# Rotary embedding in two stored parts, added on GpSimd where queries and keys are read

## Chip, cores and metric

One core of a Trainium2 chip runs one step of a hybrid layer (differential attention beside a state-space scan, then a feed-forward part). The metric is the time of one execution on the device in microseconds (us), the median of the runs.

The core has a tensor engine (TensorE, PE in the profile; PEld is its weight load), a vector engine (VectorE, DVE), a scalar engine (ScalarE, ACT), GpSimd (POOL) and SyncE (SP), which in this kernel issues nearly all DMA transfers. Each engine works through its own instructions in the order of the program and waits for the others by semaphores.

## What is computed

The part of the reference that the change touches. Queries and keys are cut out of one projection; the rotary embedding is a sum of two products, and it is made for the 1024 latent tokens alone, not for the 128 context tokens.

```python
def apply_rope(x, cos, sin):
    return x * cos + rotate_half_axial(x) * sin

proj = h @ w_in                      # columns: q | k | v | u, 512 each
q_in, keys = apply_rope(q, ...), apply_rope(k, ...)
keys = concatenate([ctx_k, keys])    # 128 cached context keys, 1024 latent keys
s = einsum(q_blk, k) * scale         # 4 heads, two maps each
p = softmax(s)
w = p[:, :, 0] - lam * p[:, :, 1]
attn = rmsnorm(einsum(w, v))
# beside it: u -> bidirectional complex scan -> gelu -> gated unit
# then: output projection, residual, feed-forward
```

## The kernel before

Tokens stand in nine tiles of 128 rows: tiles 0 to 7 are latent, tile 8 (`CH`) is the context. All matrix products are made from split operands (a high and a low part), so three products stand for one.

The input projection (`win_mm`, lines 455 to 466) goes over chunks of 256 columns in the order u, v, k, q, two chunks each, and over the nine tiles in each chunk: one step is 24 products of 128x256 into one PSUM tile, of which there are three. One step later `win_evac` (468 to 503) empties it. For values and for context rows that is a copy on ACT into `st`. For latent rows of keys and queries DVE does four things: the product with the cosines into `rt` (line 488), the two products with the sines into `st` (493, 494), and the add of the two in place (495). `st` is a ring of three tiles, `rt` a single one. The store of `st` to a scratch tensor in DRAM (`q_s`, `k_s`, `v_s`; line 498) is put in the list `later` and issued on SP in the next round; from step 49 on the evacuation stands after the first products of a step, and its store one step later.

The order of all engines' work is written out by hand: the loop at line 1318 interleaves the projection's steps with a side generator, `front_side`. While values are projected, it builds the scans' matrices; while keys and the first queries are projected, it runs the scans (`ssm_pipe`, lines 918 to 1072: transposes and products on PE, rotations and scans on DVE, adds on GpSimd at 983 and 1008); and beside the last queries it reads the keys (`kv_steps`, 1175 to 1214), followed in part by the split of the gated unit's input (line 1231).

`kv_steps` goes over ten tiles: the context's keys, the cached keys, then latent tiles 0 to 7. `load` (line 1182) fetches 256 KB into `kin`, a ring of two; `split` makes the high part on ACT (1196) and the low part on DVE (1197) and then asks for the tile after next; PE transposes the split tile (1209) and ACT copies it into the key matrix (1213). One projection step takes two such tiles.

Attention works in units (token tile, head), four to a tile. The query tile is loaded by `q_load` (1374, `qin`, a ring of two), split by `q_split` on ACT (1380) and `q_low` on DVE (1388) with two copies on GpSimd (1390), and transposed for the next tile (`q_trans`). The load of a tile is asked for in one unit, and the split comes in the unit after. Beside it the output projection's weights are split, high part on ACT (1504, `woh`) and low part on GpSimd (1505, `wol`); in a unit of the loop at line 1597 this stands ahead of `q_split`.

Of the kernel before, what the change touches and what calls it, by code (L numbers as in the profile page):

```python
# [20 lines left out]
P = 128  # L21
D = 1024
KD = D // P
ATT = 512
# [33 lines left out]
def tile_hybrid_step(  # L58
# [39 lines left out]
    q_s = [dr.tile([P, ATT], F32, name=f"q_s{t}") for t in range(NT)]  # L98
    k_s = [dr.tile([P, ATT], F32, name=f"k_s{t}") for t in range(NT)]
    v_s = [dr.tile([P, ATT], F32, name=f"v_s{t}") for t in range(NT)]  # L100
    u_c = dr.tile([P, ATT], F32, name="u_c")
# [43 lines left out]
    def rsqrt1s(pl, cols):  # L145
        """The inverse root of some columns, divided by RS."""
        ts = []
        for ss, scale, tag in cols:
            v, y, f = [pl.tile([P, 1], F32, tag=tag + n, name=tag + n) for n in "vyf"]
            yi = pl.tile([P, 1], I32, tag=tag + "i", name=tag + "i")  # L150
            ts.append([v, y, f, yi, yi.bitcast(F32)])
        for (v, y, f, yi, cur), (ss, scale, tag) in zip(ts, cols):
            if scale is None:
                V.tensor_scalar(v, ss[:, 0:1], ss[:, 1:2], EPS, ALU.add, ALU.add)
            else:
                V.tensor_scalar(v, ss, scale, EPS, ALU.mult, ALU.add)  # L156
        for v, y, f, yi, cur in ts:
            V.tensor_single_scalar(yi, v.bitcast(I32), 1, op=ALU.logical_shift_right)
        for v, y, f, yi, cur in ts:
            V.tensor_scalar(yi, yi, -1, 0x5F3759DF, ALU.mult, ALU.add)  # L160
        for c in (-3.0, -12.0, -768.0):
            for v, y, f, yi, cur in ts:
                V.tensor_scalar(f, cur, cur, v, ALU.mult, ALU.mult)  # L163
            for x in ts:
                v, y, f, yi, cur = x
                V.scalar_tensor_tensor(y, f, c, cur, ALU.add, ALU.mult)  # L166
                x[4] = y
        return [x[1] for x in ts]
# [18 lines left out]

    # ------------------------------------------------------------- pools for the first part
    pst_es, pst = pool("pst", space=PSUM)
# [17 lines left out]

    # ------------------------------------------------------------- loads
    wm_raw = {}
# [6 lines left out]
    def load_wm0(j, n):  # L216
        """Half of a quarter of the first shift's (n even) or scale's columns."""
        if j % 2 == 0:
# [94 lines left out]
    load_wm0(1, 3)  # L313
    # ------------------------------------------------------------- modulation, statistics, normalised input
    def mod_mm(ps, c0, nq, k):
# [18 lines left out]

    # ------------------------------------------------------------- statistics of the rows
    TG = [(0, 4), (4, 8), (8, 9)]
# [52 lines left out]

    # ------------------------------------------------------------- input and output maps, state on the partitions  # L390
    prm = pb.tile([P, NQ, 4, 8, GC], F32, name="prm")
# [56 lines left out]

    # ------------------------------------------------------------- input projection
    u_sb = [su.tile([P, 8, CH, GC], F32, name=f"u_sb{o}") for o in range(4)]  # L450
# [17 lines left out]
    def win_evac(c0, t, ps):  # L468
        if c0 >= 1536:
# [5 lines left out]
            else:  # L475
                st = p1c.tile([P, NW], F32, tag="st", bufs=3, name="st")
                A.copy(st, ps)
                later.append(lambda: DMA.dma_start(u_c[:, cu:cu + NW], st))
            return
        st = p1c.tile([P, NW], F32, tag="st", bufs=3, name="st")  # L480
        sec, cq = c0 // ATT, c0 % ATT
        if sec == 2 or t == CH:
            A.copy(st, ps)
        else:
            t1 = p1c.tile([P, NW], F32, tag="rt", bufs=1, name="rt")
            nh = NW // HD
# [7 lines left out]
            V.tensor_mul(s5[:, 1], p5[:, 0], r5)  # L494
            V.tensor_add(st, st, t1)
        dst = (q_s, k_s, v_s)[sec][t]
        def store():
            DMA.dma_start(dst[:, cq:cq + NW], st)
            if t == CH and sec:
                o = (None, new_k, new_v)[sec].rearrange("a b t h e -> (a b t) (h e)")  # L500
                DMA.dma_start(o[:, cq:cq + NW], st)

        later.append(store)

    # ------------------------------------------------------------- the start

# [12 lines left out]
    def mod_out(j):  # L519
        """Shifts and scales of two blocks of channels."""  # L520
        rows = mod_rows(psm0.pop(j))
# [26 lines left out]

    # small things
    ones2 = pp.tile([P, 2, NS], F32, name="ones2")  # L550
# [305 lines left out]

    # ------------------------------------------------------------- maps of the scans, four groups of a direction at a time
    def after(f):
# [57 lines left out]

    # ------------------------------------------------------------- scans, four groups at a time
    def ssm_pipe(sp, Q):
# [177 lines left out]
    class Pipe:  # L1096
        """Staggered generators: a new one every `every` steps, each moved on once a step."""

# [15 lines left out]

    # the rest of the modulation, a quarter of its columns at a time
    MSEC = (2048, 3072, 4096, 5120)
# [54 lines left out]

    # ------------------------------------------------------------- keys
    kvd = {}

    def kv_steps(ktp):
        kins = {}

        def load(t):
# [3 lines left out]
            DMA.dma_start(kin, src)  # L1182
            kins[t] = kin

        seq = [CH, -1] + list(range(CH))
# [17 lines left out]
        for n, t in enumerate(seq):  # L1203
            split(n + 1)
            ks = kss.pop(n)
            for h2 in range(2):
# [8 lines left out]

    # ------------------------------------------------------------- gated unit
    zsp = {}
# [91 lines left out]

    # ------------------------------------------------------------- the projection, with the rest beside it  # L1310
    tm_es = None
# [34 lines left out]
    p1_es.close()  # L1346
    # ------------------------------------------------------------- attention
    def rsqrt_pool(pl, ss, n, scale, tag, bufs=1, split=False):
# [23 lines left out]
    def q_load(t):  # L1372
        qin = pa.tile([P, 2 * NH, HD], F32, tag="qin", bufs=2, name="qin")
        DMA.dma_start(qin, q_s[t].rearrange("p (h e) -> p h e", e=HD))
        tl_[t] = dict(qin=qin)

    def q_split(t, late=False):
# [159 lines left out]

    # ------------------------------------------------------------- gated unit
    gl_es, gl = pool("gl", side="left")
# [17 lines left out]

    # the context's queries go beside the unit's products
    def ctx(m):
# [12 lines left out]
    for n in range(3):  # L1572
        next(gms)
        if n == 1:
            q_split(CH)
            q_load(order[2])
    for h in range(NH):
        q_trans(CH, h)
# [18 lines left out]
    for i in range(NH - 2, N):  # L1597
# [31 lines left out]
        if j < N:  # L1629
# [6 lines left out]
            if tj + 1 < NT:  # L1636
                q_trans(order[tj + 1], h)
            if h == NH - 1 and tj + 2 < NT:
                q_split(order[tj + 2], True)
            if i >= NH - 1:  # L1640
# [36 lines left out]

    # ------------------------------------------------------------- output projection, second norm
    mx_load(order[1])
# [24 lines left out]

    # quarters of the second part's input: half of the tokens, half of its columns, half of that half of tokens
    quart = [{n: slot(f"r{4 * b + i}", dt=F32) for i, n in enumerate(("A11", "A12", "A21", "A22"))} for b in range(2)]
# [73 lines left out]

    # weights of the second part's inputs: quarters, their sums, split
    raw, wop = {}, {}
# [178 lines left out]

    # ------------------------------------------------------------- feed-forward: gate and up parts
    psf_es, psf_ = pool("psf", space=PSUM)
# [13 lines left out]
    def prod(f, i, b):  # L1977
        """One of the seven products of a block, and the sums that it completes."""
        u = un.setdefault((f, b), {})
# [125 lines left out]

    # ------------------------------------------------------------- feed-forward: second product
    HEAD = 1
# [36 lines left out]

    # the seven products of a pair of rows' tiles, of columns' halves and of token tiles (q, q + 4)
    def w2_load(p):
# [5 lines left out]
    def w2_tasks(p):  # L2152
        """Sums in place and splits: rows' tiles (0, 1), columns' halves (0, 1)."""
        at = {1: (0, 0), 7: (0, 1), 2: (1, 0), 3: (1, 1), 5: (2, 0), 6: (2, 1), 4: (1, 0)}
# [68 lines left out]
    def mm2(ps, s, p, n, ix, start, stop):  # L2223
        """Passes of one product: tokens' operand ix by the rows' operand n."""
        h, l = [t[1][:, ix] if isinstance(ix, int) else t[1][:, ix[0], ix[1]] for t in g2[s]]
# [282 lines left out]
def _rope_tables():  # L2508
    """Rotary tables of the token grid (shapes alone), rows ordered as the token tiles are:
    partition p of tile j holds token p * CH + j; the sine of an axis once for both halves."""  # L2510
    tok = (np.arange(P)[:, None] * CH + np.arange(CH)[None, :])
# [30 lines left out]
```

## Time and profile before

| | us |
|---|---|
| median of three runs | 1561.98 |
| lowest and highest of them | 1559.31, 1562.66 |
| the profiled execution, span from first to last instruction | 1562.2 |
| PE busy in it | 1451.2 |
| DVE busy | 1177.3 |
| ACT busy | 677.4 |
| POOL (GpSimd) busy | 534.6 |

The profile is one execution on the chip. Its page gives the span, the busy time of each engine, and the busy tenths of each engine in 40 equal slices of the span. Further views group instructions by line, list who waited for whom, cut the span into stretches, or print instructions in order of time. A tile's name stands on the left of its inputs (`ks<-kin`). "Idle before" is the time for which an engine did nothing ahead of an instruction, and the name behind the arrow is what ended it. Rows of an engine with a "q" behind its name belong to its sequencer, which issues DMA transfers and waits.

### The profile page before, as it was taken

Reading aid. Unit: us, or ns where it says so; the run is one execution under the profiler, and the core shown is the slowest. Engines: PE = TensorE matmul, PEld = TensorE weight load, DVE = VectorE, ACT = ScalarE, POOL = GpSimd, SP = SyncE. Lnnn points to the kernel's source line nnn. Section 1 sums busy time; section 2 is a strip of 40 time slices with the busy share of each in tenths; the row PEclk is TensorE's granted clock in tenths of the full one; section 3 lists DMA queues with packets and bytes.
Section 4 is the critical chain, followed back from the end, with each engine's and each line's share of the span. In section 5 each row is a group of like instructions: output and inputs, shape, how many; then the busy total and the mean of one; then the engine's idle time right before and its main releaser. Section 6 shows DMA issues by size and latency. Waiting matters only on the chain. (4 is left out here: it accounts for less than half of the span.)

```text
span 1562.2 us, 27432 instructions
## 1 busy us (share of the span) xinstructions
PE 1451.2 (93%) x10331; PEld 1326.9 (85%) x10331; DVE 1177.3 (75%) x2049; ACT 677.4 (43%) x1381; POOL 534.6 (34%) x656
## 2 busy tenths in 40 slices
PE   4879998989999999989879999999999999999986
PEld 3867797888989999868779999999999996888765
DVE  5579839997558888648797666666666678898988
ACT  2443255542658887536652223222322236333322
POOL 1355417774113442321440000000000017786866
PEclk9879999999999999989999999999999999999998
DMA  9329944333442111055412222222222123333325
GB/s 294 117 80 334 338 156 120 109 114 111 126 147 80 48 49 35 8 159 166 121 42 75 81 79 72 67 82 78 72 67 81 58 94 106 107 115 106 123 94 189
DMA packets 162452, 175.70 MB, mean 112 GB/s; under 512 B 18080, under 2 KB 132720, under 8 KB 162320
## 3 DMA queue, kind: packets, MB, share of 16 engines
q1 hardware_dynamic: 161392, 173.24, 34.8%
q8 instruction: 82, 1.34, 0.4%
q10 hardware_dynamic: 816, 0.57, 0.1%
q0 software_dynamic: 112, 0.13, 0.1%
q14 instruction: 50, 0.41, 0.1%
HBM read 128.70 MB, written 45.20 MB: 111 GB/s over the span
## 5 line engine op out<-in xcount | busy, mean ns | idle before, releaser
L1984 PE MATMUL m<-l,wh 128*128 128x288 f32 x1320 | 276.7, 296 | 5.5 <-DVE l L1712 4.4
L1984 PE MATMUL m<-r,wh 128*128 128x288 f32 x1144 | 241.5, 297 | 3.4 <-DVE rav L156 3.0
L1984 PEld LDWEIGHTS m<-l,wh 128*128 128x128 f32 x1320 | 215.6, 189 | 6.6 <-DVE l L1712 4.9
L1984 PE MATMUL m<-l,wl 128*128 128x288 f32 x704 | 208.4, 296 | 2.9 <-DVE wl L1801 2.9
L1984 PEld LDWEIGHTS m<-r,wh 128*128 128x128 f32 x1144 | 188.0, 189 | 4.2 <-DVE r L1712 4.0
L463 PE MATMUL ps_in<-wh,hh 128*128 128x256 f32 x576 | 179.7, 312 | 5.0 <-DVE hh L385 4.1
L465 PE MATMUL ps_in<-wh,hl 128*128 128x256 f32 x576 | 167.4, 291 | 5.5 <-DVE hl L388 5.5
L464 PE MATMUL ps_in<-wl,hh 128*128 128x256 f32 x576 | 167.3, 290 | 0.7 <-DVE wl L272 0.7
L2162 POOL TENSOR_TENSOR l<-r 128x512 f32<-128x512 f32 x2 | 3.0, 1521 | 452.8 <-DMA r<-in_w_ffn_out_dram 452.8
L1984 PE MATMUL m<-r,wl 128*128 128x288 f32 x528 | 157.1, 298 | 0.2 <-DVE wl L1801 0.2
L1800 ACT CAST wh<-raw 128x512 fp32r<-128x512 f32 x132 | 77.8, 621 | 147.4 <-DVE raw L1826 117.6
L463 PEld LDWEIGHTS ps_in<-wh,hh 128*128 128x128 f32 x576 | 114.6, 199 | 25.3 <-issue 18.9
L1984 PEld LDWEIGHTS m<-l,wl 128*128 128x128 f32 x704 | 133.1, 189 | 3.1 <-DVE wl L1801 3.1
L1801 DVE TENSOR_TENSOR wl<-raw,wh 128x512 fp32r<-128x512 f32 x132 | 93.3, 708 | 38.5 <-ACT wh L1800 38.4
L465 PEld LDWEIGHTS ps_in<-wh,hl 128*128 128x128 f32 x576 | 114.4, 199 | 6.5 <-DVE hl L388 6.4
L464 PEld LDWEIGHTS ps_in<-wl,hh 128*128 128x128 f32 x576 | 115.0, 200 | 1.1 <-DVE wl L272 1.1
L1424 DVE TENSOR_REDUCE mx<-S 128x1 f32<-128x1152 f32 (+1 forms) x72 | 88.7, 1236 | 22.1 <-PE S L1421 21.8
L1984 PEld LDWEIGHTS m<-r,wl 128*128 128x128 f32 x528 | 100.3, 190 | 0.5 <-DVE wl L1801 0.4
L2264 DVE TENSOR_TENSOR acc<-acc,fo 128x1024 f32<-128x1024 f32 (+1 forms) x77 | 82.8, 1102 | 8.4 <-PE fo L2228 8.4
L1431 ACT ACTIVATE p<-S,mx 128x1152 f32<-128x1152 f32 (+1 forms) x72 | 81.1, 1127 | 13.9 <-DVE mx L1424 10.2
L1421 PE MATMUL S<-kT,qT 128*128 128x384 f32 x384 | 83.0, 351 | 0.5 <-ACT p L1431 0.5
L1008 POOL TENSOR_TENSOR Hp<-tA,tB 64x288 f32<-64x288 f32 x64 | 61.6, 963 | 30.7 <-DVE tB L969 26.3
(550 smaller groups left out, 3535.0 us busy)
## 6 DMA issues: line engine op xcount, KB each, us to landing
wm<-in_w_mod_dram SPq DMA_DIRECT2D x48, 512.0 KB
raw<-in_w_ffn_in_dram SPq DMA_DIRECT2D x88, 256.0 KB
g_s<-u SPq DMA_DIRECT2D x88, 144.0 KB
wraw<-in_w_in_dram SPq DMA_DIRECT2D x28, 256.0 KB
r<-in_w_ffn_out_dram SPq DMA_DIRECT2D x12, 512.0 KB
l<-in_w_ffn_out_dram SPq DMA_DIRECT2D x10, 512.0 KB
mat_s<-out SPq DMA_DIRECT2D x16, 288.0 KB
omat<-mat_s SPq DMA_DIRECT2D x8, 576.0 KB
```

The source lines that it names most:

```text
L463: PE.matmul(ps, la, wh, start=(k == 0), stop=False)
L464: PE.matmul(ps, la, wl, start=False, stop=False)
L465: PE.matmul(ps, lb, wh, start=False, stop=(k == KD - 1))
L1008: G.tensor_tensor(H[64 * ri:64 * ri + 64, two::2, off:off + NS], tA[s, ri], tB[s, ri], ALU.add)
L1421: PE.matmul(S[:, c, 0:cw], qT[:, 2 * h + m, j, :], K[:, 2 * h + m, c * cw:(c + 1) * cw], start=(j == 0), stop=(j == 1))
L1424: V.tensor_reduce(u["mx"][:, m:m + 1], S[:, 0:nc3, 0:cw], mybir.AxisListType.XY, ALU.max, negate=True)
L1431: A.activation(p[:, 0:nc3 * cw].rearrange("p (c n) -> p c n", n=cw), u["S"][m][:, 0:nc3, 0:cw], AF.Exp, bias=u["mx"][:, m:m + 1], scale=1. ...
L1800: A.copy(h, src)
L1801: V.tensor_sub(l, src, h)
L1984: PE.matmul(ps, w[:, k, :], a[:, k, :], start=(k == 0 and j == 0), stop=(k == 3 and j == 2))
L2162: G.tensor_tensor(x(o), x(a), x(b), ALU.subtract)
L2264: V.tensor_add(a, a, x)
```

## The change

The add on DVE (line 495) goes. The product with the cosines stays in its own tile, is stored to a scratch tensor of its own (`q_c`, `k_c`, latent tiles only), and is fetched beside the other part where keys and queries are read; GpSimd adds the two in place ahead of the split. `rt` becomes a ring of two, `st` one of two instead of three; the new tiles `kco` and `qco`, in which the cosine parts arrive, have one buffer each. Comments are taken out too, which moves the line numbers and nothing else.

```diff
+    q_c = [dr.tile([P, ATT], F32, name=f"q_c{t}") for t in range(CH)]
+    k_c = [dr.tile([P, ATT], F32, name=f"k_c{t}") for t in range(CH)]
...
 def win_evac(c0, t, ps):
...
-                st = p1c.tile([P, NW], F32, tag="st", bufs=3, name="st")
+                st = p1c.tile([P, NW], F32, tag="st", bufs=2, name="st")
...
-        st = p1c.tile([P, NW], F32, tag="st", bufs=3, name="st")
+        st = p1c.tile([P, NW], F32, tag="st", bufs=2, name="st")
         sec, cq = c0 // ATT, c0 % ATT
+        t1 = None
...
-            t1 = p1c.tile([P, NW], F32, tag="rt", bufs=1, name="rt")
+            t1 = p1c.tile([P, NW], F32, tag="rt", bufs=2, name="rt")
...
-            V.tensor_add(st, st, t1)
         dst = (q_s, k_s, v_s)[sec][t]
         def store():
             DMA.dma_start(dst[:, cq:cq + NW], st)
+            if t1 is not None:
+                DMA.dma_start((q_c, k_c)[sec][t][:, cq:cq + NW], t1)
...
 def kv_steps(ktp):
-        kins = {}
+        kins, kcs = {}, {}
...
             DMA.dma_start(kin, src)
             kins[t] = kin
+            if 0 <= t < CH:
+                kcs[t] = ktp.tile([P, 2 * NH, HD], F32, tag="kco", bufs=1, name="kco")
+                DMA.dma_start(kcs[t], k_c[t].rearrange("p (h e) -> p h e", e=HD))
+
+        def add(n):
+            if n < len(seq) and seq[n] in kcs:
+                G.tensor_tensor(kins[seq[n]], kins[seq[n]], kcs.pop(seq[n]), ALU.add)
...
         for n, t in enumerate(seq):
             split(n + 1)
+            add(n + 2)
...
 def q_load(t):
...
         tl_[t] = dict(qin=qin)
+        if t < CH:
+            qco = tl_[t]["qco"] = pa.tile([P, 2 * NH, HD], F32, tag="qco", bufs=1, name="qco")
+            DMA.dma_start(qco, q_c[t].rearrange("p (h e) -> p h e", e=HD))
+
+    def q_add(t):
+        d = tl_[t]
+        G.tensor_tensor(d["qin"], d["qin"], d.pop("qco"), ALU.add)
...
             q_split(CH)
+            q_add(order[1])
             q_load(order[2])
+            q_add(order[2])
...
             if h == NH - 1 and tj + 2 < NT:
+                q_add(order[tj + 2])
                 q_split(order[tj + 2], True)
```

## Rows read from the trace of the kernel before

**Rows 1.** The page: span, busy us, DVE busy tenths in slices of 39 us.

```profile
span 1562.2 us, 27432 instructions
...
PE 1451.2 (93%) x10331; PEld 1326.9 (85%) x10331; DVE 1177.3 (75%) x2049; ACT 677.4 (43%) x1381; POOL 534.6 (34%) x656
...
DVE  5579839997558888648797666666666678898988
```

**Rows 2.** By stretch: engines busy us, granted clock, DMA share, GB/s.

```profile
core 0: us, PE busy (x) PEld busy (x) DVE busy (x) ACT busy (x) POOL busy (x), PEclk, DMA share, GB/s
160.00:200.00 40.00, 39.72 (x401) 30.06 (x399) 30.33 (x44) 11.53 (x33) 15.52 (x12) 1.00 0.99 343
...
235.00:362.00 127.00, 108.58 (x1023) 100.03 (x1022) 121.87 (x203) 60.75 (x157) 92.03 (x127) 0.93 0.40 117
362.00:400.00 38.00, 38.00 (x354) 37.23 (x354) 22.77 (x53) 11.10 (x18) 10.63 (x16) 1.00 0.31 96
400.00:430.00 30.00, 28.56 (x255) 28.21 (x254) 18.29 (x42) 20.45 (x41) 4.08 (x4) 1.00 0.47 136
430.00:470.00 40.00, 35.88 (x223) 33.63 (x221) 21.92 (x55) 23.27 (x56) 5.36 (x7) 1.00 0.42 149
470.00:620.00 150.00, 145.80 (x1115) 140.14 (x1116) 129.04 (x179) 125.08 (x235) 61.48 (x118) 1.00 0.17 54
```

**Rows 3.** Groups of DVE, 235 to 362 us: busy us, mean ns, idle before.

```profile
L1001 DVE TENSOR_TENSOR_SCAN Ht<-dr,St 128x288 f32<-128x288 f32 x29 | 34.6, 1230 | 2.6 <-POOL St L985 2.6
L495 DVE TENSOR_TENSOR st<-st,rt 128x256 f32<-128x256 f32 x16 | 15.6, 977 | 0.6
```

**Rows 4.** Waits, 235 to 362 us: total us, times, longest us.

```profile
PE pS L977 <- DVE tB L969: 18.1, 7, 4.6
```

**Rows 5.** The add's own line: ns min/median/max, first and last start.

```profile
L495 DVE TENSOR_TENSOR st<-st,rt x32: 424/822/1053, 239.6 to 426.9; 128x256 f32<-128x256 f32 x32
```

**Rows 6.** The stores of the keys: ns of issue, first and last start.

```profile
L498 SPq DMA_DIRECT2D k_s<-st x18: 319/330/533, 240.7 to 357.3; - x18
```

**Rows 7.** ACT in order of time, 404 to 428 us: start, duration, [idle before].

```profile
407.49 0.64 ACT L1196 CAST ks<-kin 128x512 fp32r<-128x512 f32 x1
...
419.17 0.63 ACT L1196 CAST ks<-kin 128x512 fp32r<-128x512 f32 x1 [0.17 <-DMA kin<-k_s]
...
421.57 0.62 ACT L1196 CAST ks<-kin 128x512 fp32r<-128x512 f32 x1 [0.53 <-DMA kin<-k_s]
...
424.84 0.62 ACT L1196 CAST ks<-kin 128x512 fp32r<-128x512 f32 x1 [1.17 <-DMA kin<-k_s]
```

**Rows 8.** SP, issues of the loads of keys, 355 to 442 us.

```profile
403.62 0.32 SPq L1182 DMA_DIRECT2D kin<-k_s  x1
...
416.44 2.47 SPq L1182 DMA_DIRECT2D kin<-k_s  x2
...
420.67 0.32 SPq L1182 DMA_DIRECT2D kin<-k_s  x1
```

**Rows 9.** GpSimd's adds of 128x512 f32 at the end of the kernel.

```profile
L2270 POOL TENSOR_TENSOR acc<-acc x4: 1283/1307/2207, 1466.1 to 1504.5; 128x512 f32<-128x512 f32 x4
```

**Rows 10.** PE, 404 to 412 us: transposes of every other tile of keys.

```profile
405.99 0.80 PE L1209 MATMUL pk<-identr,ks 128*128 128x128 f32 x8
...
410.27 0.80 PE L1209 MATMUL pk<-identr,ks 128*128 128x128 f32 x8
```

**Rows 11.** ACT in attention, 470 to 625 us: casts of two query tiles.

```profile
483.92 0.64 ACT L1380 ACTIVATE qh<-qin 128x512 fp32r<-128x512 f32 x1
...
507.33 0.64 ACT L1380 ACTIVATE qh<-qin 128x512 fp32r<-128x512 f32 x1
```

**Rows 12.** GpSimd in attention, 505 to 511 us.

```profile
507.04 1.29 POOL L1505 TENSOR_TENSOR wol<-wor,woh 128x512 fp32r<-128x512 f32 x1 [2.92 <-ACT woh L1504]
```

**Rows 13.** DVE, 395 to 402 us: first operations of two evacuations.

```profile
396.83 0.42 DVE L488 TENSOR_TENSOR rt<-ps_in,rc 128x256 f32<-128x256 f32 x1 [4.91 <-PE ps_in L465]
...
399.71 0.42 DVE L488 TENSOR_TENSOR rt<-ps_in,rc 128x256 f32<-128x256 f32 x1 [1.00 <-PE ps_in L465]
```

## The prediction

> **What bounds the kernel now.** I read the digits by slice first: VectorE (DVE) stands at nine tenths in three slices on end, the seventh to the ninth of 39 us, 234 to 351 us [rows 1]. The table by stage then says what that is [rows 2]. From 235 to 362 us DVE works 121.87 of 127 us and TensorE (PE) 108.58, at a granted clock of 0.93: this is the projection of the keys with the scans beside it, and DVE bounds it. PE has its waits there for DVE's rotation of the scan input, 18.1 us in 7 waits [rows 4], while DVE itself waits 2.6 us for GpSimd ahead of its scans [rows 3]. From 362 us on PE is busy without a gap, or nearly so: queries' projection, the reading of the keys (400 to 430), attention (470 to 620). There, work taken from DVE is worth nothing, but a new wait in front of PE costs its whole length, since PE runs its instructions in the order in which they are written.
>
> The sum is made against the profiled execution, whose span is 1562.2 us [rows 1]; the median of the runs is 1561.98, so I add to 1562.
>
> **Removed: the add of the two rotary parts on DVE.** There are 32 of them, 16 before 362 us [rows 3] and 16 behind it. The latter lie where PE is the bound [rows 2]: worth 0. The 16 before take 15.6 us, 977 ns each [rows 3], but the shortest of this shape takes 424 ns [rows 5]; the rest goes with GpSimd, which is busy 92.03 of the 127 us [rows 2]: in the order of time one of its adds of the scan runs beside nearly every long add of DVE. So the gain lies between 16 x 0.424 = 6.8 us (if the time shared with GpSimd moves to the next operation) and 15.6 us (if it goes too). Which of the two depends on what follows an add, a rotation read from PSUM or a scan; the scans average 1230 ns, so they have such time in them already [rows 3]. Neither end is nearer, so I take the middle, 11.2 us, times DVE's share of the stage, 0.96: **-10.8 us**. PE's own idle time there (127 - 108.58 = 18.4 us) lets that through.
>
> Here a rule of the Trainium skill bears on the sum. The row shows the add at 0.42 us and at 1.05 us [rows 5]. GPSIMD Engine Reference, section "Key points", says that GpSimd shares its SBUF interfaces with VectorE and contends with DVE instructions that have two SBUF inputs. By that rule the shared time is not the add's own: it goes to the next DVE operation with two SBUF inputs, and the gain is the low end. That result is rival (a) below.
>
> **Moved out: the stores.** Each of the 32 evacuations writes two tiles, so 32 more stores of 128 KB, and 16 more loads of 256 KB where the parts are read. The DMA share is 0.31 to 0.47 in the stretches from 235 to 430 us [rows 2]: taken at 0. The ring of `st` goes from three tiles to two and `rt` now waits for a store to land rather than for DVE. An evacuation meets its own buffer two steps later; the tightest steps are 2.88 us apart [rows 13], so 5.8 us, against about 1 us of evacuation, 0.7 us for two issues and 2.7 to 3.1 us from issue to use (below). That cover is about 1 us, and PSUM's three tiles stand behind it: 0. In the stretch 160 to 200 us the DMA engines are at 0.99 [rows 2], and how long a store takes there no row tells; if it took over two steps, ScalarE (ACT), which evacuates the values, would wait. I take 0, with +4 us as the upper end (half a microsecond in each of some 8 steps).
>
> **Added: reading the keys.** Eight tiles of keys come in two parts, and the second part (`kco`) has one buffer. Its load for tile m therefore waits on SyncE (SP) until GpSimd's add for tile m-1 has read it; behind that wait on SP are the stores of the queries and the next loads, and for the add wait ACT's cast, DVE's low part and PE's transposes. This makes a loop: load, add, next load. Its load: keys issued at 416.44 are cast at 419.17, and those issued at 416.44 + 2.47 - 0.32 = 418.59 at 421.57 [rows 7, 8], with ACT idle before both, so 2.73 and 2.98 us. Its add, 128x512 of f32 on GpSimd: 1283 ns at the least, 1307 at the median of one group [rows 9]. So the loop takes 4.0 to 4.4 us, in the middle 4.2, by tile. Before, seven periods lie between the first and the last latent tile's cast, 407.49 and 424.84 [rows 7]: 2.48 us each, which is PE's pace, as two tiles and one step of products take 4.28 us [rows 10]. The loop is 1.7 us slower by tile: 7 x 1.72 = 12.0 us. The first tile: its second part is issued 0.4 us behind the 403.62 of the first [rows 8], is used from 406.8, and the add ends at 408.1 instead of a cast at 407.49, +0.6. Sum **+12.6 us**. Nothing covers it, because PE has 28.56 busy of 30 us there [rows 2] and its next products stand behind the transposes. Bounds: 7 x 1.5 = +10.5; and with loads as late as the last one (issued 420.67, cast 424.84, 4.2 us) for some of the tiles, +18.
>
> **Added: reading the queries.** The first two latent tiles are added while the gated unit still runs, GpSimd being idle most of 430 to 470 (5.36 us busy of 40) [rows 2]: 0, at most +2 if the second's load lands behind the values' loads. Six more come inside attention. In five of them the queue of GpSimd has a weight's low part (`wol`) just ahead: at 507.04 it starts, for 1.29 us, and ACT's cast of the queries starts at 507.33 [rows 11, 12]; the other four show the same 0.3 us. The new add follows, 508.33 to 509.6, and the cast, which now needs it, starts 2.3 us later. Behind it on ACT are the copies of the transposed weights of attention, on DVE the low part and the next maximum; PE needs both. From 470 to 620 PE is idle 4.2 us in 150 [rows 2], 0.65 us in a tile of 23.4 (from cast to cast [rows 11]), so it can take back perhaps 0.5: 1.8 us x 5 = **+9.0 us**. Bounds: 0 if ACT (24.9 us idle in the same stretch) makes it up before PE is touched, 2.5 x 5 = +12.5 with the slower adds. The sixth, the last one, has no weight ahead: 0.
>
> **Sum.** 1562 - 10.8 + 12.6 + 9.0 = 1572.8: about **1573 us**, 0.7% slower. The low ends give 1562 - 15.6 + 10.5 + 0 = 1557, the high ends 1562 - 6.8 + 18 + 12.5 + 6 = 1592.
>
> **Rivals.**
> (a) The time shared with GpSimd stays on DVE and goes to the scan or the subtraction that comes next. Then the gain is 6.8 us and the time 1562 - 6.8 + 21.6 = 1577. For it: the add next to an idle GpSimd is short. Against: many an add is followed by rotations out of PSUM.
> (b) Both ends balance: the whole 15.6 us comes back and attention takes the hold at half price (4.5): 1562 - 15.6 + 12.6 + 4.5 = 1563.5. For it: ACT's idle time in attention. Against: ACT is followed at once by copies that PE waits for.
> (c) Faster: the adds at the reading ends are hidden by work that stands in front of PE. The place is PE's queue before the transposes of keys and queries. It decides from the point where the loop of `kco` is not over 2.48 us a tile and the late cast stays inside ACT's idle time; then the price of both ends is 0 to 5 us and the time is 1562 - 10.8 + 0 to 5 = 1551 to 1556. For it: attention's transposes of a tile come one unit (a quarter of a tile, 5.9 us) behind its cast. Against: 2.73 + 1.28 is far over 2.48, and a single buffer leaves no load ahead.
> (d) The change doesn't relieve DVE at all, since the scans wait for GpSimd instead [rows 3]: 1562 + 21.6 = 1584. Against: 2.6 us of such waits only.
>
> **How the numbers follow.** Forecast 0.50, (a) 0.17, (b) 0.13, (c) 0.15, (d) 0.05. A measurement of this kernel can tell about 0.2%, 3 us, from no change. Faster: (c), and the quicker part of (b), 0.17. Same: most of (b) and the lowest edge of the forecast, 0.12. Slower: the rest, 0.71. The range leaves out the faster half of (c) and the highest ends: 1554 to 1584.
>
> **What would show it.** Scan stage: the first and the last store of keys, 240.7 and 357.3 [rows 6], come 7 to 15 us closer together, DVE still at 0.95 or more. Keys: casts 4.0 to 4.4 us apart, ACT waiting for GpSimd, SP's load of `kco` waiting for GpSimd, PE idle a third or more of that stretch. Attention: five waits of ACT for the query add, 2 to 2.5 us each, and PE's gaps behind them. What would prove me wrong: casts still 2.5 us apart (the loop is not there), or no gaps of PE behind the late casts, or an unchanged distance of the key stores.

## The result and the profile after

The changed kernel takes 1583.1 us (median of 4 runs, 1577.19 to 1586.12), the kernel before 1560.88 us on the same chip: ratio 1.0135, 95% interval 1.012 to 1.015. That is +22 us where +11 was predicted, on the predicted side and inside the range, near its upper end. The profiled execution, the longest of the four (1586.12 us), has a span of 1584.4 us, 22.2 more than the 1562.2 of before [rows 1], so the two traces show the difference of the medians.

To see where it arises, pair PE's instructions of the two traces in the order of PE's queue (10331 in each) and subtract the starts. The changed kernel's PE is 1.0 us late at 232 us, ahead of the scan stage, and 7.5 us early at 400; 9.25 us late at 430, 10.6 at 470, 23.7 to 23.8 from 592 to 650, and 22.1 at the end. So (in the times of the kernel before):

| stretch | predicted | shift in the trace |
|---|---|---|
| up to 235 us | 0 | +1.0 |
| scan stage, 235 to 400 us | -10.8 | -8.5 |
| reading the keys, 400 to 430 us | +12.6 | +16.8 |
| gated unit, 430 to 470 us | 0 | +1.3 |
| reading the queries, 470 to 620 us | +9.0 | +13.2, five holds 11.65 of it |
| behind 620 us | 0 | -1.6 |
| sum (rounded) | +10.8 | +22.1 |

The last line is no more than kernels that are equal behind 620 us differ by: the kernel with the smaller ring alone (the last experiment) shows -2.0 there.

The same stretches as [rows 2], of the changed kernel. Columns as there: stretch, length, busy us of PE, PE's weight loads, DVE, ACT and GpSimd with their instructions, granted clock, DMA share, GB/s.

```profile
235.00:362.00 127.00, 114.94 (x1123) 106.50 (x1124) 118.56 (x199) 63.57 (x163) 100.50 (x132) 0.97 0.48 139
...
400.00:430.00 30.00, 23.16 (x159) 22.19 (x158) 8.90 (x18) 13.93 (x28) 13.14 (x11) 0.77 0.54 164
430.00:470.00 40.00, 34.42 (x194) 32.99 (x193) 16.61 (x44) 20.44 (x48) 7.17 (x7) 0.87 0.44 160
470.00:620.00 150.00, 135.60 (x998) 127.16 (x997) 119.00 (x166) 112.99 (x214) 65.94 (x109) 0.99 0.19 62
```

The scan stage got denser: PE is 114.94 us busy where it had 108.58. Behind it PE has holes that were not there: 23.16 of 30 us in the reading of the keys (28.56 before) and 135.60 of 150 in attention (145.80 before), and the granted clock, 1.00 in all three stretches before, is 0.77 and 0.87 in the first two.

**The scan stage.** DVE's groups from 235 to 362 us, as in [rows 3]: line, operation, operands, count, busy us, mean ns, idle ahead of it and what ended that.

```profile
L1006 DVE TENSOR_TENSOR_SCAN Ht<-dr,St 128x288 f32<-128x288 f32 x32 | 36.6, 1183 | 4.0 <-POOL St L990 4.0
L972 DVE TENSOR_TENSOR tA<-Ht,E 128x576 f32<-128x576 f32 x16 | 15.1, 943 | 0.6
L972 DVE TENSOR_TENSOR tA<-pS,E 128x576 f32<-128x576 f32 x14 | 10.5, 749 | 3.9 <-POOL Hp L1013 3.9
L275 DVE TENSOR_TENSOR wl<-wraw,wh 128x512 fp32r<-128x512 f32 x8 | 9.7, 1211 | 0.0
L973 DVE TENSOR_TENSOR tB<-Ht,E 128x288 f32<-128x288 f32 x16 | 9.0, 564 | 0.0
...
L974 DVE SCALAR_TENSOR_TENSOR tB<-pS,E 128x288 f32<-128x288 f32 x15 | 6.7, 445 | 0.0
L973 DVE TENSOR_TENSOR tB<-pS,E 128x288 f32<-128x288 f32 x14 | 6.2, 445 | 0.0
```

The groups of the kernel before that answer to them, so far as [rows 3] does not have them:

```profile
L967 DVE TENSOR_TENSOR tA<-Ht,E 128x576 f32<-128x576 f32 x14 | 10.6, 758 | 0.5
L967 DVE TENSOR_TENSOR tA<-pS,E 128x576 f32<-128x576 f32 x14 | 10.5, 748 | 1.5 <-PE pS L977 1.5
L272 DVE TENSOR_TENSOR wl<-wraw,wh 128x512 fp32r<-128x512 f32 x8 | 9.1, 1138 | 0.0
...
L968 DVE TENSOR_TENSOR tB<-Ht,E 128x288 f32<-128x288 f32 x14 | 6.3, 452 | 0.0
```

The add is gone, 15.6 us of DVE. The rotations of `Ht`, which read two tiles of SBUF, have become longer (`tA` 758 to 943 ns, `tB` 452 to 564 ns); the same rotations of `pS`, which read one operand from PSUM, have not (748 to 749, 445 to 445). The longer mean is a mixture of two kinds. Seven of the 16 large rotations of `Ht` run beside an add of GpSimd now and take 1174 to 1187 ns; nine run beside none and take 757 to 759, as all but the last did before. One of the seven, the GpSimd adds beside it, and the same rotation before, when GpSimd had finished (duration in the second column):

```profile
311.92 1.18 DVE L972 TENSOR_TENSOR tA<-Ht,E 128x576 f32<-128x576 f32 x1
```

```profile
310.00 2.48 POOL L1013 TENSOR_TENSOR Hp<-tA,tB 64x288 f32<-64x288 f32 x2
```

```profile
316.38 0.76 DVE L967 TENSOR_TENSOR tA<-Ht,E 128x576 f32<-128x576 f32 x1
```

The rotations of `pS` mostly run beside GpSimd's adds too, in both kernels, and take 740 to 758 ns each. Paired one by one, the rotations of `Ht` are 3.7 us longer in all and the eight operations of `wl` 0.6 us: 4.3 us of the add's time have moved there. And DVE now waits 4.0 + 3.9 = 7.9 us for GpSimd, where it waited 2.6 us [rows 3]. PE's waits for the rotation (`pS <- tB`: total, times, longest) fell from 18.1 us [rows 4] to 11.6 us:

```profile
PE pS L982 <- DVE tB L974: 11.6, 7, 3.8
```

At 362 us PE is 10.2 us earlier than at 235. It loses 1.7 of that at products with the scans' last output, which now wait for GpSimd (`Hp`); before, they waited for nothing:

```profile
368.03 0.43 PE L1048 MATMUL yc<-omat,Hp 128*32 128x128 f32 x8 [1.56 <-POOL Hp L1023]
```

The stores of the keys answer [rows 6] (ns of issue, first and last start): they are 110.6 us apart where they were 116.6, so 6.0 closer, just under the 7 to 15 that the prediction asked for. DVE is at 118.56 of 127 us, 0.93, where it asked for 0.95.

```profile
L501 SPq DMA_DIRECT2D k_s<-st x18: 319/406/998, 240.6 to 351.2; - x18
```

**The reading of the keys.** ACT's casts, as in [rows 7]: start, duration, idle ahead and its end. The first is the first of all tiles, the next lines the first, second and last latent tile.

```profile
394.55 0.62 ACT L1208 CAST ks<-kin 128x512 fp32r<-128x512 f32 x1 [5.10 <-DMA kin<-k_s]
...
401.54 0.62 ACT L1208 CAST ks<-kin 128x512 fp32r<-128x512 f32 x1 [1.45 <-POOL kin L1195]
...
405.64 0.62 ACT L1208 CAST ks<-kin 128x512 fp32r<-128x512 f32 x1 [2.51 <-POOL kin L1195]
...
431.66 0.62 ACT L1208 CAST ks<-kin 128x512 fp32r<-128x512 f32 x1 [2.34 <-POOL kin L1195]
```

(431.66 - 401.54) / 7 = 4.30 us a tile, where before it was 2.48. The reason stands in GpSimd's adds and SP's issues of the same stretch:

```profile
400.22 1.29 POOL L1195 TENSOR_TENSOR kin<-kin,kco 128x512 f32<-128x512 f32 x1 [32.24 <-DMA kco<-k_c]
404.35 1.26 POOL L1195 TENSOR_TENSOR kin<-kin,kco 128x512 f32<-128x512 f32 x1 [2.84 <-DMA kco<-k_c]
408.77 1.28 POOL L1195 TENSOR_TENSOR kin<-kin,kco 128x512 f32<-128x512 f32 x1 [3.17 <-DMA kco<-k_c]
```

```profile
401.53 0.32 SPq L1191 DMA_DIRECT2D kco<-k_c  x1
402.91 0.32 SPq L1187 DMA_DIRECT2D kin<-k_s  x1
405.64 0.32 SPq L1191 DMA_DIRECT2D kco<-k_c  x1
```

The loop can be read off: the add of 400.22 ends at 401.51, the next load of `kco` is issued at 401.53, lands for an add at 404.35 (2.82 us later), which ends at 405.61, and the next load is issued at 405.64. SP waits seven times for GpSimd there, 10.3 us in all, as the prediction asked for. PE is idle 27% of the time between the first and the last latent cast (22.03 us busy of 30.12), somewhat less than the third that it asked for.

The granted clock (third number from the end) in stretches of 5 us, with PE's busy us behind the stretch's length:

```profile
400.00:405.00 5.00, 4.55 (x41) 4.17 (x39) 0.69 (x1) 1.69 (x4) 1.95 (x2) 1.00 0.63 208
405.00:410.00 5.00, 2.87 (x19) 2.90 (x20) 1.42 (x4) 2.01 (x4) 1.83 (x2) 0.82 0.49 153
...
415.00:420.00 5.00, 3.90 (x21) 3.93 (x22) 2.17 (x5) 2.77 (x7) 2.65 (x3) 0.50 0.66 165
...
435.00:440.00 5.00, 5.00 (x23) 5.00 (x23) 1.97 (x4) 2.02 (x5) 0.00 (x0) 0.61 0.15 53
440.00:445.00 5.00, 5.00 (x31) 5.00 (x30) 3.07 (x8) 3.38 (x8) 0.00 (x0) 1.00 0.20 76
...
455.00:460.00 5.00, 5.00 (x25) 4.90 (x25) 0.14 (x1) 1.86 (x5) 0.00 (x0) 0.66 1.04 387
```

PE works with holes, the clock falls from 1.00 (2.4 GHz) to 0.50 (1.2 GHz) for a whole stretch, and it is back at 1.00 only from 440 us, when the holes are over. It falls twice more, to 0.66 in the gated unit (455 to 460) and to 0.83 in attention (480 to 490). Before, it was 1.00 from 400 to 620 us [rows 2].

**Attention.** One of the five casts of queries that answer [rows 11] (ACT waits 10.7 us in all five, 2.14 each), with GpSimd's work ahead of it, which answers [rows 12], and what PE then waits for:

```profile
523.99 0.63 ACT L1400 ACTIVATE qh<-qin 128x512 fp32r<-128x512 f32 x1 [2.14 <-POOL qin L1395]
```

```profile
521.45 1.27 POOL L1525 TENSOR_TENSOR wol<-wor,woh 128x512 fp32r<-128x512 f32 x1 [2.92 <-ACT woh L1524]
522.68 1.27 POOL L1395 TENSOR_TENSOR qin<-qin,qco 128x512 f32<-128x512 f32 x1
```

```profile
525.04 0.55 PE L1475 MATMUL pw<-ident,p 128*128 128x128 f32 x3 [1.48 <-ACT wT L1476]
```

One tile of attention, from cast to cast, is 25.73 us now (first line) and was 23.42 (second line):

```profile
523.99:549.72 25.73, 23.42 (x176) 22.02 (x176) 20.81 (x28) 19.82 (x38) 12.53 (x21) 1.00 0.19 54
```

```profile
507.33:530.75 23.42, 22.94 (x178) 22.01 (x178) 20.18 (x28) 19.81 (x38) 10.67 (x21) 1.00 0.15 46
```

PE is idle 2.31 us in it where it was 0.48; ACT does the same 19.8 us of work in both.

### The profile page after: what moved, and what is told of

The parts are those of the page before. It is cut to its first block, busy times and chain, and to the rows that moved or that the text cites. A ratio compares the mean times of both kernels' runs of the same rounds, so it can differ in the third digit from the quotient of the medians.

```text
span 1584.4 us, 27491 instructions
## 1 busy us (share of the span) xinstructions
PE 1459.3 (92%) x10331; PEld 1332.3 (84%) x10331; DVE 1159.0 (73%) x2017; ACT 678.5 (43%) x1381; POOL 561.8 (35%) x672
## 5 line engine op out<-in xcount | busy, mean ns | idle before, releaser
L1013 POOL TENSOR_TENSOR Hp<-tA,tB 64x288 f32<-64x288 f32 x64 | 66.8, 1044 | 22.8 <-DVE tB L974 19.9
```

Source lines behind the costliest of these rows:

```text
L1013: G.tensor_tensor(H[64 * ri:64 * ri + 64, two::2, off:off + NS], tA[s, ri], tB[s, ri], ALU.add)
```

## Experiments

Each ran beside the kernel before on the same chip; that one's median was 1560.36 us (15 runs) for the first four and 1560.24 us (18 runs) for the others.

**Only the keys' adds taken out of the kernel before.** What does the removal bring by itself, with no store and no load added?

```diff
-            V.tensor_add(st, st, t1)
+            if sec == 0:
+                V.tensor_add(st, st, t1)
```

> The kernel before, with the 16 adds of the keys' two rotary parts left out (the keys lack their cosine part); no store, load or GpSimd add takes their place. Theory: the adds were worth about 8 us and not 15.6, since part of the time shared with GpSimd moves to the rotations and scans behind them, and since DVE then waits more for GpSimd: 8 us faster, about 1553. Rival: the adds were worth more, and the stores of the second part took the difference back: 11 to 15 us faster, 1546 to 1550.

Measured: 1553.2 us (7 runs), ratio 0.9951 (0.9934 to 0.9969), so 7.2 us less, and PE 9.2 us early at 400 us, 1.3 of it from ahead of the scan stage, so 7.9 in the stage. DVE's groups of the scan stage:

```profile
L1002 DVE TENSOR_TENSOR_SCAN Ht<-dr,St 128x288 f32<-128x288 f32 x31 | 36.3, 1208 | 3.3 <-POOL St L986 3.3
L968 DVE TENSOR_TENSOR tA<-Ht,E 128x576 f32<-128x576 f32 x16 | 15.1, 943 | 0.6
L968 DVE TENSOR_TENSOR tA<-pS,E 128x576 f32<-128x576 f32 x14 | 10.5, 750 | 4.8 <-POOL Hp L1009 2.5 <-POOL Hp L1019 2.0 <-PE pS L978 0.4
```

The same 943 ns for the rotation of `Ht` and the same waits for GpSimd (3.3 + 4.5 us) as in the changed kernel. So the removal gives 7 to 8 us, not 15.6 and not 0, and what it fails to give is not due to the new stores.

**The change for the keys alone.** The queries are added on DVE as before and come in one part.

```diff
+            if sec == 0:
+                V.tensor_add(st, st, t1)
+                t1 = None
...
-        if t < CH:
+        if False:
...
-            q_add(order[1])
...
-            q_add(order[2])
...
-                q_add(order[tj + 2])
```

> Only the keys are stored in two parts; the queries are summed on DVE at their evacuation as before. Theory: the scan stage gives 8 us, the single buffer of the second part costs about 17 us in the reading of the keys, attention is as before: about 9 us slower than before, 1570. Rival: the holds in attention were a follow-up of the late keys and not of the query adds; then nearly all of the 22 us stays: 1580.

Measured: 1569.42 us (9 runs), ratio 1.0046 (1.0029 to 1.0063). Casts of the latent tiles run from 399.16 to 429.14 us, 4.28 us apart; PE is 9.2 us early at 400 and 6.9 us late at 430 us. The keys' side alone loses more (16.0 us) than the scan stage gains (8.2, with 1.0 of the 9.2 from ahead of it).

**The change for the queries alone.** The keys are added on DVE and come in one part.

```diff
+            if sec == 1:
+                V.tensor_add(st, st, t1)
+                t1 = None
...
-            if 0 <= t < CH:
+            if False:
```

> Only the queries are stored in two parts; the keys are summed on DVE at their evacuation as before. Theory: the 16 adds taken from DVE behind 362 us are worth 0, the five holds of ACT in attention cost 2.3 us each, about 12 us in all: 1573. Rival: TensorE makes the holds up when it isn't late from the keys already: 1561 to 1565.

Measured: 1573.3 us (4 runs), ratio 1.0074 (1.0055 to 1.0093). The five holds are there, and from 470 to 620 us PE loses 11.4 us; in the 235 us ahead of that it loses 0.9.

```profile
ACT qh L1403 <- POOL qin L1398: 10.7, 5, 2.2
```

The reading of the keys has PE at 28.52 of 30 us and the clock at 1.00. By the medians the two halves add up within the intervals: +9.1 and +12.9 are +22.0, the whole change.

**The keys' second part gets a place of its own by tile**, in the tile's still unused columns of the key matrix, so that its load waits for no add. The load then goes in runs of 512 bytes in place of 2 KB, and the add's operands are grouped to match; all else is the changed kernel.

```diff
-                kcs[t] = ktp.tile([P, 2 * NH, HD], F32, tag="kco", bufs=1, name="kco")
-                DMA.dma_start(kcs[t], k_c[t].rearrange("p (h e) -> p h e", e=HD))
+                kcs[t] = kvd["l"].bitcast(F32)[:, 0:NH, (t + 1) * P:(t + 2) * P]
+                DMA.dma_start(kcs[t], k_c[t].rearrange("p (h e) -> p h e", e=P))
...
-                G.tensor_tensor(kins[seq[n]], kins[seq[n]], kcs.pop(seq[n]), ALU.add)
+                k = kins[seq[n]].rearrange("p (a b) e -> p a (b e)", b=2)
+                G.tensor_tensor(k, k, kcs.pop(seq[n]), ALU.add)
```

> As the changed kernel, but the second part of each tile of keys is loaded into that tile's own columns of the key matrix, which are written later anyway: eight buffers in place of one, the same loads, adds and stores (runs of 512 bytes in place of 2 KB). Theory: the loop of load, add, next load is the cost. Without it a tile waits only for its first part's ring of two, 1.4 + 3.0 + 1.3 us for two tiles, 2.9 us a tile in place of 4.3: about 11 us faster than the changed kernel, 1572. Rival: the adds on GpSimd and the doubled loads themselves are the cost: the casts stay some 4 us apart, and the time stays at 1580 or over.

Measured: 1573.43 us (4 runs), ratio 1.0078 (1.0055 to 1.0101). Casts from 398.77 to 423.03 us, 3.47 us apart; the reading of the keys now costs 11.1 us of PE's time (10.7 early at 400, 0.4 late at 430) where it cost 16.8. So the single buffer's loop is a cause. It is not all of it: 3.47 is over the 2.9 expected and still 1 us over the 2.48 of before, and the next suspect is the first part, `kin`: it has two buffers, and GpSimd now holds each 1.3 us longer.

**The queries' add ahead of the weight.** The same instructions, but GpSimd is given the add before `wol` of the same unit.

```diff
+        if j < N and units[j][1] == NH - 1 and order.index(units[j][0]) + 2 < NT:
+            q_add(order[order.index(units[j][0]) + 2])
         if i >= 4 and i % NH != 3 and wn < 2 * KD:
             wo_split(wn // 2, wn % 2)
...
-                q_add(order[tj + 2])
```

> As the changed kernel, but in attention GpSimd adds a query tile ahead of the weight's low part that stands in the same unit, not behind it. Theory: each of the five holds is the weight's low part (1.27 us) plus the add's end; ahead of it the add waits for the load alone, and a hold falls from 2.15 to some 0.5 us: 8 us faster than the changed kernel, about 1575. Rival: the load lands too late for that, or any hold of ACT costs the same: within 3 us of the changed kernel, 1580 to 1584.

Measured: 1572.93 us (4 runs), ratio 1.0079 (1.0061 to 1.0096), 10 us under the changed kernel. The waits of ACT and GpSimd from 480 to 650 us:

```profile
POOL qin L1395 <- DMA qco<-q_c: 7.1, 2, 3.6
...
ACT qh L1400 <- POOL qin L1395: 3.1, 2, 1.6
```

Two holds of 1.5 us are left of five of 2.14, and those two wait for the load and not for the weight. PE loses 4.3 us from 470 to 620 us where it lost 13.2: three of the five tiles are as long as before, the two with a hold are 2.1 and 2.3 us longer. The place in GpSimd's queue is what the holds were made of.

**The keys alone, with a place of its own and three buffers of `kin`,** loads one tile further ahead. It is the second experiment's kernel with the fourth's edit, and:

```diff
-            kin = ktp.tile([P, 2 * NH, HD], F32, tag="kin", bufs=2, name="kin")
+            kin = ktp.tile([P, 2 * NH, HD], F32, tag="kin", bufs=3, name="kin")
...
+        load(seq[2])
...
-            if n + 2 < len(seq):
-                load(seq[n + 2])
+            if n + 3 < len(seq):
+                load(seq[n + 3])
```

> Only the keys in two parts, the second in the tile's own columns of the key matrix, and the first in a ring of three, so that three loads are under way. The queries as before. Theory: the gain of the scan stage (8 us) is kept and the reading of the keys costs only the later first tile, about 2 us: 6 us faster than before, 1555. Rival: GpSimd's adds between load and cast cost more than the ring hides, and nothing is gained: 1561 or over.

Measured: 1552.3 us (6 runs), ratio 0.9955 (0.9941 to 0.9969): faster than both kernels. The reading of the keys, and the first and the last latent cast (18.11 us apart, 2.59 a tile):

```profile
400.00:430.00 30.00, 27.85 (x211) 27.29 (x209) 18.81 (x35) 19.89 (x42) 12.94 (x10) 1.00 0.46 144
```

```profile
395.84 0.62 ACT L1213 CAST ks<-kin 128x512 fp32r<-128x512 f32 x1 [0.58 <-POOL kin L1199]
...
413.95 0.63 ACT L1213 CAST ks<-kin 128x512 fp32r<-128x512 f32 x1
```

PE is 12.3 us early at 400 (4.4 of it from ahead of the scan stage) and 10.8 from 430 to 650 us. GpSimd adds the keys as in the changed kernel, and their second part is stored and loaded in the same amount: the cost of reading them in two parts was the rings, not the add and not the traffic.

**All 32 adds left out of the kernel before.**

```diff
-            V.tensor_add(st, st, t1)
```

> The kernel before, with all 32 adds of the two rotary parts left out (keys and queries lack their cosine part). Theory: the 16 adds of the queries stand where TensorE is the bound, so this is within 1 us of the kernel that leaves out the keys' adds alone, about 1553. Rival: they are worth as much as they take, 8 us: 1545.

Measured: 1550.89 us (5 runs), ratio 0.995 (0.9933 to 0.9968). Against 1553.2 without the keys' adds this is no difference that the intervals can tell: the queries' 16 adds were worth nothing, as the prediction had it. It is also what the kernel could win at most by the adds, and the kernel with three buffers has it within the interval.

**The smaller ring alone.**

```diff
-                st = p1c.tile([P, NW], F32, tag="st", bufs=3, name="st")
+                st = p1c.tile([P, NW], F32, tag="st", bufs=2, name="st")
...
-        st = p1c.tile([P, NW], F32, tag="st", bufs=3, name="st")
+        st = p1c.tile([P, NW], F32, tag="st", bufs=2, name="st")
```

> The kernel before with two tiles in place of three in the ring into which the projection is evacuated, and nothing else. Theory: a store has landed before its tile is wanted again two steps later, also between 160 and 200 us where the DMA engines are full: within 1 us of before. Rival: ScalarE waits for stores there: 2 to 4 us slower.

Measured: 1561.42 us (10 runs), ratio 1.0006 (0.9996 to 1.0016): 0, also between 160 and 200 us, where the DMA engines are at 0.99: PE's shift does not change there. The +1.0 us of the first line of the table is therefore no effect of the ring; the two kernels that only lack adds, and are the kernel before up to there, have PE 1.3 and 3.9 us early at 235 us.

## Why the prediction was right and where it was short

**The bound and the sign: right.** DVE bounded the scan stage and nothing else that the change touches. A part of the work taken from it came back there, and work put in front of PE behind 400 us cost its whole length. Rival (c) fell with the casts 4.3 us apart, rival (b) with a relief far under 15.6 us and with PE's holes behind the late casts of the queries. The measured time lies at that of rival (d), 1584 us, but not by its mechanism: (d) has no relief of DVE, and the relief is there, 6 to 8.5 us by three ways of looking at it (the shift with 8.5, the stores of the keys with 6.0, the adds' removal by itself with 7.2). The size was forecast at half: +10.8 by the sum, +22 measured. That it still lies inside the range is in part luck: the range's high ends stood for slower loads and adds and for waits for stores, and about half of what used them up, 5.6 us, was the clock, of which the sum had no term.

**Scan stage, -10.8 predicted, -8.5 in the trace.** The step that was off is the choice of the middle between the bounds 6.8 and 15.6. The add's shared time went partly to later operations, and GpSimd's own pace took a part: 15.6 less 4.3 (rotations and weights) less 5.3 (7.9 instead of 2.6 us of waits for GpSimd), with 1.5 us of DVE's waits for PE gone and 29 scans, paired, 1.2 us shorter, is 8.7 us. So it is a mixture of rivals (a) and (d), and the forecast lay above it. The rule weighed in the prediction (the Trainium skill, GPSIMD Engine Reference, section "Key points": GpSimd contends with DVE instructions that have two SBUF inputs) is borne out in kind: of two rotations of one size the one with two SBUF inputs took up to 1187 ns beside an add of GpSimd in place of 758, and the one with a PSUM input stayed at 749 beside such adds. What it was made to say, that all of the shared time would move on, does not hold: the add's share above its 424 ns was 8.8 us, and 4.3 us of such time came back.

**Reading the keys, +12.6 predicted, +16.8 in the trace.** The loop was sized rightly: 4.30 us a tile for 4.2, which makes 30.12 - 17.35 = 12.8 us over seven periods for 12.0; the second experiment has 4.28. Two terms were mis-sized or missing. The first latent tile was taken at +0.6; it came 6.99 us behind the first cast where before it came 5.24 us (rows of the two traces), +1.75. And behind the last cast the sum had nothing: the last store of queries is issued 437.49 - 431.66 = 5.8 us after it, before 429.1 - 424.84 = 4.3 us, PE being at 0.71 and 0.61 of its clock there. That is 1.6 of the 2.2 us that are left. What the rest is can be seen in 32 instructions of PE, from the transposes of the last tile on (426.3 to 430.5 us of the kernel before). PE has no wait between them in any of the kernels, and before they took 4.14 us at a clock of 1.00:

| kernel | shift, 400 to 430 us | of it first tile and loop | rest | the 32 instructions, us | clock in them |
|---|---|---|---|---|---|
| the change | 16.8 | 14.5 | 2.2 | 6.57 | 0.56 |
| keys alone | 16.0 | 13.6 | 2.4 | 6.71 | 0.55 |
| own place | 11.1 | 9.1 | 2.0 | 6.33 | 0.59 |
| add ahead | 14.4 | 14.7 | -0.3 | 4.14 | 1.00 |
| own place, three buffers | 1.5 | 1.6 | 0 | 4.14 | 1.00 |

So the rest is the clock: the same products without a wait take 2.2 to 2.6 us longer where it is low, and there is no rest where it is back. The queries' add ahead of the weight changes nothing in this stretch, and that kernel has the same loop (casts 4.28 us apart); its stretch behind the last cast, at 427.00 us, is

```profile
430.00:435.00 5.00, 5.00 (x33) 5.00 (x32) 3.31 (x8) 4.13 (x12) 0.00 (x0) 1.00 0.21 75
```

Every kernel with the single buffer's loop shows the cost of the loop; the 2.2 us behind it come or don't come, and what decides between the two isn't shown.

**Gated unit, 0 predicted, +1.3.** The adds of the first two query tiles were hidden, as predicted. The loss isn't that of the low clock up to 440 us, which lies in the stretch before; it lies in the second fall, 455 to 461 us: 31 instructions of PE, without a wait between them, take 6.34 us at 0.73 where before they took 4.78 at 1.00. With the second part in a place of its own they take 6.37, also at 0.73; with the keys alone, the queries alone or the add ahead 4.78 to 4.79 at 1.00. The sum had no term for the clock.

**Reading the queries, +9.0 predicted, +13.2.** The hold itself was right, 2.14 us five times for a predicted 2.3, with the weight's low part ahead of it as the cause, which the moved add confirmed; no hold at the sixth. The step that failed is "it can take back perhaps 0.5". A tile became 2.31 us longer for a hold of 2.14: the idle time that PE had in a tile is still there. It lies at other waits of PE in the tile (0.39 us ahead of the transposes of the output, unchanged, and 0.09, now 0.43, for DVE's `osb`), and the 1.48 us of the hold's own wait come on top. Five holds make 11.65 us; the other 1.5 us lie at the beginning of attention, where the clock falls a third time: 30 instructions of PE, without a wait between them, take 5.20 us at 0.67 (483.3 to 488.5 us) for 3.63 before. The queries alone, the own place and the add ahead have 1.00 and 3.62 to 3.63 us there.

**Stores and rings, 0 predicted: right**, by the smaller ring alone (1.0006) and by the kernel with three buffers, which has all the keys' additional traffic and loses nothing. DVE did wait once for a store of `rt` to land, 5.3 us at 371 us, more than the cover of about 1 us that the prediction had worked out; PE's shift does not change there.

The steps that were off are thus three: the relief of DVE taken at the middle, a hold priced at its length less a saving, and no term for the clock, whose three falls make 2.4 + 1.6 + 1.6 = 5.6 of the 22.1 us in this trace. The kernel's four times, 1577.19 to 1586.12 us, spread by 9 us; how much of that is the clock isn't shown, since one execution was profiled. What was left open too: two buffers for `kco` in its own pool weren't tried.

## What to carry to other kernels

Before moving an operation to an idle engine at the place where its result is read, write down the loop of buffers there (load, operation, next load) and the place in the engine's queue: here they cost 16.0 us for the keys and 11.4 for the queries, where the operation's removal gave 7 to 8; with own places and a ring of three the keys' half of the move wins 0.45% where it lost 0.46%. Price a hold in front of a saturated PE at its length or somewhat more (2.14 us cost 2.31, and 1.5 us cost 2.1 and 2.3), and take no idle time off unless it lies behind the hold. What DVE gained by losing work that it did beside GpSimd lay between the unshared and the whole duration of that work, near the lower end (7 to 8.5 of 6.8 to 15.6 us): look at which operation with two SBUF inputs will then run beside GpSimd, and at the next wait for GpSimd.

## What the runs showed of the hardware that was not expected

Contention followed the operand's place, not the operation: beside an add of GpSimd, the rotation 128x576 took 1174 to 1187 ns from SBUF (757 to 759 without one) and 740 to 758 ns with one operand in PSUM, and the add of 128x256 had taken up to 1053 ns for 424. When the add was removed, about half of its shared time (4.3 of 8.8 us) reappeared in operations with two SBUF inputs.

Holes of about 2 us in PE's work, one in each 4.3 us, took the granted clock down to 0.50 of 2.4 GHz for a 5 us stretch in which PE was busy 3.90 us, and it was not back at 1.00 before 440 us, 8 us behind the last late cast. Waits in front of PE so can have a price beyond their length, here 2.2 to 2.6 us behind the eight waits in three kernels and none in a fourth with the same eight waits, in which the clock was back at 1.00 when they were over.
